# Attention inside a fused transformer block: output products issued one step later, two banks for transposed weights, three one-bank score tiles, two gates dealt out by halves

## The chip, the cores and the metric

The kernel runs on one NeuronCore of one Trainium2 chip. The metric is the time of one execution in microseconds, as the device measures it. Beside it stands one profiled execution, from which all traces here come. Engines are named as the profile names them: PE (TensorE, matrix products; PEld is its weight load), DVE (VectorE), ACT (ScalarE), POOL (GpSimd) and SP (SyncE, which only issues transfers here).

## The reference

One layer of a hybrid encoder, on 1024 tokens of 1024 channels, in float32. Cut to what matters:

```python
h    = rmsnorm(x, g_pre_mix)
proj = h @ w_in                                  # [u_pool 512 | q 512 | k 512 | v 512]
y_pool = multiscale_pool(u_pool, ...) @ w_br_pool
# stick-breaking attention, 8 heads of 64, strictly causal
z    = (q @ k.T) * 64 ** -0.5
A[t,s] = sigmoid(z_ts) * prod_{s<j<t} (1 - sigmoid(z_tj))      # s < t
y_sb = (A @ v) @ w_br_sb
gates  = sigmoid(h @ w_gate + b_gate)            # 2048 channels
merged = gates[:1024] * y_pool + gates[1024:] * y_sb
x = x + rmsnorm(merged @ w_out, g_post_mix)
x = x + rmsnorm(relu(rmsnorm(x, g_pre_mlp) @ w_up) ** 2 @ w_down, g_post_mlp)
```

## The kernel before, in words

Every float32 operand of a product is split into a high and a low part of a narrower type (`hi` by a cast on ACT, `lo` by a subtraction on DVE), and a product is three matmuls: hi·hi, lo·hi, hi·lo (`mm3`, lines 108 to 114; a row of L110 or L112 is the first of the three). Activations lie with channels on the 128 partitions and tokens along the row, in two halves of 512 tokens. Weights come as 128x1024 tiles through `prep` (L76 load, L82 cast, L83 subtraction).

Stages, in order:

1. **phase_in** (0 to 78 us): x is loaded and split unnormalized; the sums of squares go through a matmul with a matrix of ones (`stats`, tile `ms`, L332), then `rstd` (L153 Ln and L154 Exp on ACT, L155 to L157 on DVE) makes the row factors `rb[h]` of each half, and four transposes of `rb[h]` (tile `rt`, L336) with a copy (L337) make the same factors per column. `u` (tiles `du`, `zu`), then the first q and k and the pooling mixer (`win`, `dm`, `yscr`) follow. `u_out` (L380) multiplies a finished u product with `rb` and frees its bank.
2. **phase_attention** (78 to 503 us): for each of 8 heads, four groups g = 3, 2, 1, 0 of two query blocks i = 2g and 2g+1. `att_scores` makes the scores z of one block (w = 128(i+1) columns, two matmuls for each piece of up to 512), T = sigmoid(z) and F = sigmoid(-z) on ACT (L551, L552), a running product over F on DVE (L559, the scan) and its product with T (L560), which is the attention row block. F has one buffer, so the F of a block waits for L560 of the block before. `att_out` of the group before then goes through its steps m = 0..g: transposes of the weights (tile `at`, L576), a split into `ahi` (ACT, L583) and `alo` (DVE, L584), and four matmuls into `o` (L589: ahi twice, alo twice); at the end of a group `o` is folded into `oT` (L593, L594).
   Between these, `pump` deals out the head's **fillers**: steps of the gate products (`dg`, three matmuls a step, 8 steps for each half gate), of the next q and k (`dqk`) and of v (`dv`). `self.fill` lists which fillers belong to which head: head 4 has two gates (32 steps), heads 5, 6 and 7 have 48.
3. **phase_post** and **phase_mlp** (503 us to the end): branch products, output projection, norms, and the MLP by a seven-product scheme.

PSUM has eight banks of 128x512 f32. Before: `d` two, score tiles `z` two of two banks each, `o` one, `at` one.

What sets the order: the code is written in one sequence, and a list scheduler at build time reorders instructions between engines by its own estimates; within an engine the built order is then fixed. While `pin` is set, the first matmul of a triple is held behind the fourth last entry of `marks` (scores, transposes, output products).

The lines that the change and the prediction's steps touch:

Of the kernel before, what the change touches and what calls it, by code (L numbers as in the profile page):

```python
# [29 lines left out]
P = 128  # L30
# [19 lines left out]
class Block:  # L50
# [118 lines left out]
    def build(self):  # L169
# [78 lines left out]
    def phase_in(self):  # L248
# [81 lines left out]
        def stats(h):  # L330
            ms = self.zps.tile([P, H], F32, name="ms", tag="at" if h == 0 else "o", bufs=1)
            nc.tensor.matmul(ms, self.ones, accs[h], start=True, stop=True)  # L332
            self.rstd(ms, pa, ("sq", 3), out=self.rb[h])
            rt = self.zps.tile([P, H], F32, name="rt", tag="at", bufs=1)
            for j in range(4):
                nc.tensor.transpose(rt[:, j * P : j * P + P], self.rb[h][:, j * P : j * P + P], self.eye)  # L336
# [70 lines left out]
        def pool_mix(g, cur):  # L407
# [6 lines left out]
            for h in range(2):  # L414
                c = slice(h * H, h * H + H)
                d = self.zps.tile([P, H], F32, name="dm", tag=("o", "at")[h], bufs=1)
# [111 lines left out]
    def att_scores(self, h, i):  # L528
# [9 lines left out]
        z = self.zps.tile([P, 1024], F32, name="z", tag="z", bufs=2)  # L538
        pieces = [(0, max(256, min(H, w)))]
        if w > H:  # L540
            pieces.append((H, max(256, w - H)))
        tt = slice(i * P, i * P + P)
        for c, n in pieces:
            m = nc.tensor.matmul(z[:, c : c + n], q[:, tt], k[:, c : c + n], start=True, stop=False)  # L544
            if c == 0:
                self.marks.append(m)
            nc.tensor.matmul(z[:, c : c + n], qs[:, tt], k[:, c : c + n], start=False, stop=True)  # L547
# [3 lines left out]
        nc.scalar.activation(tl[:, :w], z[:, :w], AF.Sigmoid)  # L551
        nc.scalar.activation(f[:, :w], z[:, :w], AF.Sigmoid, scale=-1.0)  # L552
# [10 lines left out]
    def att_out(self, h, g, a):  # L563
# [3 lines left out]
        hd = (h % 4) * P  # L567
        for m in range(g + 1):
            diag = m == g
            at = self.zps.tile([P, H], F32, name="at", tag="at", bufs=1)  # L570
# [14 lines left out]
            for part in (hi, lo):  # L585
                for s, c in ((2 * m + 1, 0), (2 * m, 256)):
                    v = self.v[(h // 4, s)].rearrange("p h x -> p (h x)")[:, hd : hd + P]
                    first = m == 0 and c == 0 and part is hi
                    t = nc.tensor.matmul(o, v, part[:, c : c + 256], start=first, stop=diag and c == 256 and part is lo)  # L589
            self.marks.append(t)  # L590
# [22 lines left out]
    def phase_attention(self):  # L613
# [6 lines left out]
        self.w_out = 2.3  # L620
        self.pin = True
# [34 lines left out]
        self.att_out(*prev)  # L656
        while self.queue:
            self.advance()
# [645 lines left out]
```

## Time and profile before

| | |
|---|---|
| time, median of 3 runs | 1307.06 us (1303.7 to 1307.58) |
| profiled execution | 1308.59 us, of which the trace's span is 1306.8 us |
| PE busy | 1278.9 us (98%) |
| DVE busy | 915.6 us (70%) |
| ACT busy | 600.7 us (46%) |
| POOL busy | 173.8 us (13%) |
| mean granted PE clock | 0.993 |

PE is busy 98% of the span. Idle time of PE is what the trace shows directly; beside it the column PEclk of a stage tells whether PE ran at its full clock there. DVE, ACT and POOL only count where PE waits for them. Matmul ends are modelled in the trace (pipelined matmuls overlap), so rates are read from start to start: 0.23 us for a 128x512 matmul, 0.12 us for a 128x256 one.

### The profile page before, as it was taken

The page shows a single profiled execution, that of the slowest core. Times are in us where ns is not written, and L with a number is a line of the kernel's source. Part 1 is how long each engine was busy: PE and PEld are TensorE (multiplying, and loading weights), DVE is VectorE, ACT ScalarE, POOL GpSimd, SP SyncE. Part 2 cuts the span into 40 slices and gives each one's busy share as a digit, 9 for nine tenths or more (in the row PEclk, how much of TensorE's full clock was granted, in tenths as well). Part 3 has the DMA queues.
Part 4 walks back from the last instruction along what each step waited for, and adds up shares of the span by engine and source line. Part 5 has one row for each costly group of instructions (what it writes and reads, how often), then busy time and mean ns, then how long its engine had stood idle before and what let it go on. Part 6 is the DMA issues. An engine that isn't in the chain of part 4 may idle for free.

```text
span 1306.8 us, 16746 instructions
## 1 busy us (share of the span) xinstructions
PE 1278.9 (98%) x6145; PEld 1066.9 (82%) x6145; DVE 915.6 (70%) x1239; ACT 600.7 (46%) x925; POOL 173.8 (13%) x346
## 2 busy tenths in 40 slices
PE   9999999998999999999999999999999999999996
PEld 6888888887888888888878878888888888888886
DVE  8785587676777765663586869877775655776976
ACT  7244455544555543223355646544465433344341
POOL 1002213201212331100001001211121000001100
PEclk9998999999999999999999999999999999999998
DMA  6243635623746979543156667765559555556741
GB/s 221 71 155 113 204 103 155 136 66 73 154 147 191 251 230 240 166 170 104 54 188 229 189 227 251 251 229 184 188 211 354 180 185 202 193 178 240 241 166 65
DMA packets 75746, 233.72 MB, mean 179 GB/s; under 512 B 8624, under 2 KB 11184, under 8 KB 73488
## 3 DMA queue, kind: packets, MB, share of 16 engines
q1 hardware_dynamic: 47936, 143.64, 33.5%
q0 software_dynamic: 27152, 88.49, 22.7%
q8 instruction: 48, 0.79, 0.2%
q10 hardware_dynamic: 576, 0.52, 0.1%
q14 instruction: 34, 0.28, 0.1%
HBM read 178.10 MB, written 83.89 MB: 200 GB/s over the span
## 4 chain that ended last, share of the span: by engine, by line
PE 84%; DVE 8%; ACT 3%; DMA 2%; issue 2%; POOL 1%; SPq 0%; DVEq 0%; ACTq 0%; POOLq 0%
PE d L113 19%; PE d L114 19%; PE d L112 19%; PE dg L110 4%; PE dg L113 4%; PE dg L114 4%; PE o L589 2%; PE at L576 2%; DVE F L559 2%; DVE T L560 1%; PE dqk L114 1%; PE dqk L113 1%; DMA yscr<-win 1%; PE z L547 1%; PE z L544 1%
## 5 line engine op out<-in xcount | busy, mean ns | idle before, releaser
L113 PE MATMUL d<-blo,whi 128*128 128x512 f32 (+1 forms) x456 | 172.7, 379 | 0.0
L114 PE MATMUL d<-bhi,wlo 128*128 128x512 f32 (+1 forms) x456 | 171.9, 378 | 0.0
L112 PE MATMUL d<-bhi,whi 128*128 128x512 f32 (+1 forms) x456 | 168.6, 378 | 0.0
L559 DVE TENSOR_TENSOR_SCAN F<-F,past 128x896 f32<-128x896 f32 (+3 forms) x64 | 87.6, 1369 | 46.9 <-ACT F L552 46.5
L82 ACT CAST whi<-wraw 128x512 fp32r<-128x512 f32 (+1 forms) x88 | 67.6, 797 | 86.4 <-PE d L113 37.5
L110 PE MATMUL dg<-hT_hi,whi 128*128 128x512 f32 x256 | 105.3, 411 | 0.0
L114 PE MATMUL dg<-hT_hi,wlo 128*128 128x512 f32 x256 | 101.0, 394 | 0.0
L113 PE MATMUL dg<-hT_lo,whi 128*128 128x512 f32 x256 | 100.7, 393 | 0.0
L83 DVE TENSOR_TENSOR wlo<-wraw,whi 128x512 fp32r<-128x512 f32 (+1 forms) x88 | 77.8, 907 | 30.5 <-ACT whi L82 30.3
L114 PEld LDWEIGHTS d<-bhi,wlo 128*128 128x128 f32 x456 | 85.8, 188 | 16.1 <-issue 0.2
L113 PEld LDWEIGHTS d<-blo,whi 128*128 128x128 f32 x456 | 85.7, 188 | 16.1 <-issue 0.2
L112 PEld LDWEIGHTS d<-bhi,whi 128*128 128x128 f32 x456 | 85.5, 188 | 16.1
L584 DVE TENSOR_TENSOR alo<-at,ahi 128x512 fp32r<-128x512 f32 (+1 forms) x80 | 50.3, 629 | 43.2 <-ACT ahi L583 42.5
L113 PE MATMUL d<-b_lo,whi 128*128 128x512 f32 x196 | 76.7, 392 | 0.0
L112 PE MATMUL d<-b_hi,whi 128*128 128x512 f32 x196 | 75.7, 391 | 0.0
L114 PE MATMUL d<-b_hi,wlo 128*128 128x512 f32 x196 | 75.3, 392 | 0.1
L1071 DVE TENSOR_TENSOR wlo<-slots_hi,whi 128x1024 fp32r<-128x1024 f32 x29 | 35.5, 1225 | 53.8 <-ACT whi L1069 53.8
L1069 ACT CAST whi<-slots_hi 128x1024 fp32r<-128x1024 f32 x29 | 30.5, 1052 | 84.6 <-PE d L113 64.7
L583 ACT CAST ahi<-at 128x512 fp32r<-128x512 f32 (+1 forms) x80 | 43.5, 544 | 47.5 <-PE at L576 44.2
L1069 ACT CAST whi<-slots_lo 128x1024 fp32r<-128x1024 f32 x27 | 28.4, 1052 | 72.9 <-PE d L113 59.2
L1071 DVE TENSOR_TENSOR wlo<-slots_lo,whi 128x1024 fp32r<-128x1024 f32 x27 | 33.0, 1222 | 36.7 <-ACT whi L1069 36.7
L114 PEld LDWEIGHTS dg<-hT_hi,wlo 128*128 128x128 f32 x256 | 48.3, 189 | 10.5
(305 smaller groups left out, 3325.9 us busy)
## 6 DMA issues: line engine op xcount, KB each, us to landing
wraw<-w SPq DMA_DIRECT2D x80, 512.0 KB, 4.2
wscr<-w POOLq DMA_DIRECT2D x24, 1024.0 KB, 10.3
ext_b<-ascr SPq DMA_DIRECT2D x40, 512.0 KB, 4.4
gscr<-gs POOLq DMA_DIRECT2D x32, 256.0 KB, 4.1
gate<-gscr POOLq DMA_DIRECT2D x16, 512.0 KB, 3.7
pscr<-p SPq DMA_DIRECT2D x32, 256.0 KB, 3.6
braw<-w SPq DMA_DIRECT2D x16, 512.0 KB, 5.5
ascr<-c POOLq DMA_DIRECT2D x32, 256.0 KB, 5.1
```

The lines of the kernel that those rows point to most:

```text
L82: nc.scalar.copy(hi[:, c], raw[:, c])
L83: self.last_lo = nc.vector.tensor_sub(lo[:, c], raw[:, c], hi[:, c].bitcast(F32)).ins
L110: nc.tensor.matmul(ps, wh, rh, start=first and i == 0, stop=False)
L112: nc.tensor.matmul(ps, wh, rh, start=first and i == 0, stop=False)
L113: nc.tensor.matmul(ps, wh, rl, start=False, stop=False)
L114: nc.tensor.matmul(ps, wl, rh, start=False, stop=last and i == n - 1)
L559: nc.vector.tensor_tensor_scan(fr, fr, past, 1.0, ALU.mult, ALU.max)
L576: t = nc.tensor.transpose(at[:, b * P : b * P + P], a[tt][:, s * P : s * P + P], self.eye)
L583: nc.scalar.copy(hi[:, c0:], at[:, c0:])
L584: nc.vector.tensor_sub(lo[:, c0:], at[:, c0:], hi[:, c0:].bitcast(F32))
L1069: last_split[0] = nc.scalar.copy(hi, src).ins
L1071: last_split[1] = nc.vector.tensor_sub(lo, src, hi.bitcast(F32)).ins
```

## The change

Five things change.

- **Output products one step later.** The four `o` matmuls of a step are no longer issued at the end of that step. `att_out` keeps them as `pending`, and the next step (of the same group or of the next one) issues them through `att_products` after its own transposes, fillers and split. Folding `o` into `oT` moves along. After the last group an explicit `pump` and `att_products` finish.
- **`at` has two banks**, so transposes of a step can be written while those of the step before are still being split.
- **`z` is three tiles of one bank** instead of two of two banks. A block with w > 512 becomes two tiles, and the order is now matmuls, T and F of the first 512 columns, then matmuls, T and F of the rest. The scan still runs over the whole row.
- **Consequences in phase_in**: of the six u accumulators that used the score banks, three take `z` tiles and one an `at` bank; `ms` and `rt` of both halves now share the single `o` bank; `dm` of the second half may use either `at` bank.
- **Gates 4 and 12 by halves**: the first half of gate 4 moves from head 5 to head 4, the first half of gate 12 from head 6 to head 5. Head 4 has 40 filler steps, head 5 still 48, head 6 has 40.

```diff
-            4: [("g", 3), ("g", 11)],
-            5: [("q", 3), ("k", 3), ("g", 4)],
-            6: [("g", 12), ("g", 5), ("g", 13)],
+            4: [("g", 3), ("g", 11), ("g", 4, 0)],
+            5: [("g", 4, 1), ("q", 3), ("k", 3), ("g", 12, 0)],
+            6: [("g", 12, 1), ("g", 5), ("g", 13)],
...
         def stats(h):
-            ms = self.zps.tile([P, H], F32, name="ms", tag="at" if h == 0 else "o", bufs=1)
+            ms = self.zps.tile([P, H], F32, name="ms", tag="o", bufs=1)
...
-            rt = self.zps.tile([P, H], F32, name="rt", tag="at", bufs=1)
+            rt = self.zps.tile([P, H], F32, name="rt", tag="o", bufs=1)
...
-        z0 = self.zps.tile([P, 1024], F32, name="zu0", tag="z", bufs=2)
-        z1 = self.zps.tile([P, 1024], F32, name="zu1", tag="z", bufs=2)
         d2 = [self.dps.tile([P, H], F32, name="du", tag="d") for _ in range(2)]
-        dst = [d2] + [[z[:, h * H : h * H + H] for h in range(2)] for z in (z0, z1)]
+        zu = [self.zps.tile([P, H], F32, name="zu", tag="z", bufs=3) for _ in range(3)]
+        zu.append(self.zps.tile([P, H], F32, name="zu", tag="at", bufs=2))
+        dst = [d2, zu[:2], zu[2:]]
...
+        for c in range(0, w, H):
+            n = min(H, w - c)
+            cols = slice(c, c + max(256, n))
+            z = self.zps.tile([P, H], F32, name="z", tag="z", bufs=3)
+            zz = z[:, : max(256, n)]
+            m = nc.tensor.matmul(zz, q[:, tt], k[:, cols], start=True, stop=False)
+            if c == 0:
+                self.marks.append(m)
+            nc.tensor.matmul(zz, qs[:, tt], k[:, cols], start=False, stop=True)
+            nc.scalar.activation(tl[:, c : c + n], z[:, :n], AF.Sigmoid)
+            nc.scalar.activation(f[:, c : c + n], z[:, :n], AF.Sigmoid, scale=-1.0)
...
-            at = self.zps.tile([P, H], F32, name="at", tag="at", bufs=1)
+            at = self.zps.tile([P, H], F32, name="at", tag="at", bufs=2)
...
             nc.vector.tensor_sub(lo[:, c0:], at[:, c0:], hi[:, c0:].bitcast(F32))
-            for part in (hi, lo):
-                for s, c in ((2 * m + 1, 0), (2 * m, 256)):
...
-            self.marks.append(t)
+            self.att_products()
+            self.pending = (h, g, m, o, hi, lo)
+
+    def att_products(self):
+        if self.pending is None:
+            return
+        h, g, m, o, hi, lo = self.pending
+        self.pending = None
+        diag = m == g
+        for part in (hi, lo):
+            for s, c in ((2 * m + 1, 0), (2 * m, 256)):
...
+        self.marks.append(t)
+        if not diag:
+            return
...
         self.att_out(*prev)
+        self.pump(self.w_out)
+        self.att_products()
```

How the built order moves, at three places. A name with a number is one tile; the bracket names the engines for which an instruction has to wait.

PE in head 4, just after the first scores of the head, before: transposes of a diagonal step, nine filler matmuls, scores, and then that step's four products.

```order
L576 MATMUL at_2961<-eye_159,T_2770 128x128 [waits PE_49]
L576 MATMUL at_2961<-eye_159,T_2748 128x128
...
L114 MATMUL dg_3005<-hT_hi0_249,wlo_2599 128x512
L544 MATMUL z_3062<-k4_2595,q4_2467 128x512 [waits Activation_49]
L547 MATMUL z_3062<-k4_2595,qs4_2588 128x512
L544 MATMUL z_3062<-k4_2595,q4_2467 128x256
L547 MATMUL z_3062<-k4_2595,qs4_2588 128x256
L589 MATMUL o_2931<-ahi_2962,v0_3_1040 128x256 [waits Activation_49,Pool_49]
L589 MATMUL o_2931<-ahi_2962,v0_2_1068 128x256
L589 MATMUL o_2931<-alo_2963,v0_3_1040 128x256 [waits DVE_49,Pool_49]
```

The same step after: `at_3007` are its transposes, `o_2974` with `ahi_3008` and `alo_3009` its products.

```order
L575 MATMUL at_3007<-eye_159,T_2810 128x128 [waits PE_49]
...
L547 MATMUL z_3068<-k4_2635,q4_2501 128x512
L550 MATMUL z_3068<-k4_2635,qs4_2628 128x512
L575 MATMUL at_3097<-eye_159,T_2952 128x128 [waits DVE_49]
...
L547 MATMUL z_3073<-k4_2635,q4_2501 128x512 [waits Activation_49]
...
L600 MATMUL o_2974<-ahi_3008,v0_3_1048 128x256 [waits Activation_49,Pool_49]
L600 MATMUL o_2974<-ahi_3008,v0_2_1076 128x256
L600 MATMUL o_2974<-alo_3009,v0_3_1048 128x256 [waits DVE_49,Pool_49]
L547 MATMUL z_3128<-k4_2635,q4_2501 128x512 [waits Activation_49]
```

Between the transposes and the first alo product stood 9 filler and 4 score matmuls and the two ahi products; now another step's transposes, 24 `dv` and 24 `dg` matmuls, score matmuls and another step's products stand there too.

ACT at the first two-tile block of head 0, before: one T and one F over 1024 columns, F behind DVE.

```order
L551 ACTIVATE T_888<-z_883 128x1024
L496 ACTIVATE v0_2_1068<-dv_1043,rcol_167 128x4x64 [waits PE_49]
L496 ACTIVATE v0_1_1096<-dv_1071,rcol_167 128x4x64 [waits PE_49]
L552 ACTIVATE F_889<-z_883 128x1024 [waits DVE_49,Activation_49]
L551 ACTIVATE T_1132<-z_1127 128x640 [waits PE_49]
```

After: two of each.

```order
L551 ACTIVATE T_888<-z_890 128x512
L496 ACTIVATE v0_2_1076<-dv_1051,rcol_167 128x4x64 [waits PE_49]
L551 ACTIVATE T_888<-z_895 128x512 [waits PE_49]
L552 ACTIVATE F_889<-z_890 128x512 [waits DVE_49,Activation_49]
L552 ACTIVATE F_889<-z_895 128x512
```

Each block of more than 512 columns has one T and one F more on ACT, 64 instructions in all; where the second score tile comes later, its T stands behind the F of the first.

PE in phase_in, at the end of the u products, before: `ms_463` (the sums of the second half) stands among the u products, and the transposes `rt_471` of its row factors come 28 u matmuls and four transposes later.

```order
L332 MATMUL ms_463<-acc_292,ones_152 128x512 [waits DVE_49,PE_49]
L114 MATMUL zu0_331<-hT_hi1_290,wlo_188 128x512
...
L336 MATMUL rt_421<-eye_159,rb0_165 128x128 [waits DMAHW1_49,DVE_49]
L336 MATMUL rt_421<-eye_159,rb0_165 128x128 x3
L112 MATMUL zu1_332<-hT_hi1_290,whi_190 128x512
...
L114 MATMUL zu1_332<-hT_hi1_290,wlo_191 128x512
L336 MATMUL rt_471<-eye_159,rb1_166 128x128 [waits DVE_49,PE_49]
L336 MATMUL rt_471<-eye_159,rb1_166 128x128 x3
L112 MATMUL du_544<-hT_hi0_249,whi_484 128x512 [waits DVE_49,Activation_49]
```

After:

```order
L336 MATMUL rt_423<-eye_159,rb0_165 128x128 [waits DMAHW1_49,DVE_49]
L336 MATMUL rt_423<-eye_159,rb0_165 128x128 x3
...
L112 MATMUL zu_336<-hT_hi1_290,whi_190 128x512
L332 MATMUL ms_465<-acc_292,ones_152 128x512 [waits DVE_49]
L113 MATMUL zu_336<-hT_lo1_291,whi_190 128x512
L114 MATMUL zu_336<-hT_hi1_290,wlo_191 128x512
L336 MATMUL rt_473<-eye_159,rb1_166 128x128 [waits DVE_49]
L336 MATMUL rt_473<-eye_159,rb1_166 128x128 x3
L112 MATMUL du_546<-hT_hi0_249,whi_486 128x512 [waits DVE_49,Activation_49]
```

`ms_465` now stands behind the first half's transposes and copy (the shared `o` bank), and two matmuls separate it from `rt_473`, which needs its result.

More of the change, by code (lines that the diff above doesn't have):

```diff
@@ L415, in pool_mix @@
                 c = slice(h * H, h * H + H)
-                d = self.zps.tile([P, H], F32, name="dm", tag=("o", "at")[h], bufs=1)
+                d = self.zps.tile([P, H], F32, name="dm", tag=("o", "at")[h], bufs=h + 1)
                 self.mm3(d, [(wmh[:, g, :], wml[:, g, :], ph[:, c], pq[:, c])])
@@ L537, in att_scores @@
         w = (i + 1) * P
[L538 to L547, printed above, removed]
         odd = i // 2 % 2
@@ L584, in att_out @@
             nc.vector.tensor_sub(lo[:, c0:], at[:, c0:], hi[:, c0:].bitcast(F32))
[L585 to L590 removed]
+            self.att_products()
+            self.pending = (h, g, m, o, hi, lo)
+    def att_products(self):
+        nc = self.nc
+        if self.pending is None:
[3 more added lines that the diff above has]
+        diag = m == g
+        hd = (h % 4) * P
+        for part in (hi, lo):
+            for s, c in ((2 * m + 1, 0), (2 * m, 256)):
+                v = self.v[(h // 4, s)].rearrange("p h x -> p (h x)")[:, hd : hd + P]
+                first = m == 0 and c == 0 and part is hi
+                t = nc.tensor.matmul(o, v, part[:, c : c + 256], start=first, stop=diag and c == 256 and part is lo)
+        self.marks.append(t)
+        if not diag:
+            return
         b = 64 * (h % 2)
```

5 lines of the change are left out of this document (2 added, 3 removed).

## The prediction

> **What bounds the kernel now.** I read the page's first part, then PE in stages (the table of windows), then who PE waited for, then the timeline at the places those name.
>
> ```profile
> PE 1278.9 (98%) x6145; PEld 1066.9 (82%) x6145; DVE 915.6 (70%) x1239; ACT 600.7 (46%) x925; POOL 173.8 (13%) x346
> ```
>
> PE is the bound, so the change, which keeps every matmul, can only win what PE loses by standing still or by running at half clock. The windows of the attention stage (columns: length, then busy us of PE, PEld, DVE, ACT, POOL, then the granted PE clock) say how much that is:
>
> ```profile
> 104.20:107.60 3.40, 1.55 (x9) 1.06 (x8) 2.02 (x1) 2.99 (x5) 1.36 (x2) 1.00 0.00 0
> 107.60:111.00 3.40, 2.16 (x9) 1.95 (x10) 2.94 (x5) 1.62 (x2) 0.52 (x2) 0.50 0.00 0
> 111.00:114.40 3.40, 3.40 (x18) 3.40 (x18) 3.30 (x4) 1.14 (x2) 1.32 (x1) 0.50 0.00 0
> ...
> 310.00:319.20 9.20, 7.75 (x40) 6.23 (x38) 7.30 (x7) 4.32 (x8) 2.78 (x4) 1.00 0.19 39
> 319.20:322.60 3.40, 1.60 (x9) 1.22 (x10) 3.02 (x3) 0.83 (x2) 0.00 (x0) 1.00 1.12 204
> 322.60:326.00 3.40, 3.40 (x12) 2.82 (x11) 0.88 (x2) 0.59 (x1) 0.00 (x0) 0.50 0.44 79
> ...
> 360.00:503.00 143.00, 142.31 (x742) 120.68 (x741) 94.58 (x130) 70.27 (x126) 40.55 (x87) 1.00 0.74 206
> sum 425.00, PE 413.43 PEld 355.32 DVE 291.51 ACT 209.97 POOL 97.24; mean PE 37.58 PEld 32.30 DVE 26.50 ACT 19.09 POOL 8.84
> ```
>
> From 78 to 503 us PE is idle 425.00 - 413.43 = 11.6 us. Twice, right after a 3.4 us window in which PE was busy less than half (1.55 and 1.60 us), the clock falls to 0.50, for two windows and for one. Late in attention (360 on) almost nothing is lost, so there is nothing to win there. Who PE waited for:
>
> ```profile
> PE o L589 <- DVE alo L584: 4.7, 9, 1.4
> PE z L544 <- ACT F L552: 3.1, 4, 1.9
> PE at L576 <- DVE T L560: 2.3, 1, 2.3
> ```
>
> These are 10.1 of the 11.6 us, in 14 stops. One of each kind, PE with the DVE or ACT row that made it late:
>
> ```profile
> 105.60 0.50 PE L544 MATMUL z<-k,q 128*128 128x512 f32 x1 [0.81 <-ACT F L552]
> 108.84 0.47 PE L576 MATMUL at<-eye,T 128*128 128x128 f32 x1 [2.28 <-DVE T L560]
> 305.45 2.02 DVE L559 TENSOR_TENSOR_SCAN F<-F,past 128x896 f32<-128x896 f32 x1 [0.85 <-ACT F L552]
> 306.27 0.40 PE L589 MATMUL o<-ahi,v 128*128 128x256 f32 x2
> 307.39 0.53 DVE L584 TENSOR_TENSOR alo<-at,ahi 128x384 fp32r<-128x384 f32 x1
> 308.07 0.47 PE L589 MATMUL o<-alo,v 128*128 128x256 f32 x2 [1.39 <-DVE alo L584]
> 318.74 0.81 ACT L552 ACTIVATE F<-z 128x768 f32<-128x768 f32 x1 [1.85 <-DVE T L560]
> 319.60 0.50 PE L544 MATMUL z<-k,q 128*128 128x512 f32 x1 [1.86 <-ACT F L552]
> ```
>
> The third to sixth rows are the disease that the change treats: `alo` sits behind a 2.02 us scan on DVE, and PE, having nothing between, waits 1.39 us. From 306.27 to 308.07 two matmuls of 0.12 us pass: 1.80 - 0.24 = 1.56 us are lost, 0.17 more than the idle shown, since ends are modelled. So 14 stops cost 14 x 0.17 = 2.4 us more. Half clock costs half of PE's busy time in the three windows at 0.50: (2.16 + 3.40 + 3.40)/2 = 4.5 us. Waits too short to show stretch the alo products:
>
> ```profile
> L589 PE MATMUL o<-alo,v 128*128 128x256 f32 x160 | 34.8, 299 | 4.9 <-DVE alo L584 4.7
> L589 PE MATMUL o<-alo,v x160: 277/283/388, 130.3 to 501.6; 128*128 128x256 f32 x160
> ```
>
> Mean 299 against median 283 ns, x 160 = 2.6 us. All that attention loses: 11.6 + 2.4 + 4.5 + 2.6 = **21.1 us**. That is the ceiling of the gain.
>
> **The change part by part.**
>
> *Products one step later, two `at` banks.* No matmul is added; `at` writes can run ahead by one step. The distance on PE between a step's last transpose and its first alo product, counted in the built order at 0.23, 0.12 and (transposes) 0.09 us a matmul, has a mean of 3.6 us before and 8.0 after, its smallest value 1.0 before and 4.0 after. What has to fit into it is a cast, a subtraction, and at worst one scan ahead of them:
>
> ```profile
> L583 ACT CAST ahi<-at 128x512 fp32r<-128x512 f32 x48 | 28.1, 585 | 42.9 <-PE at L576 41.9
> L584 DVE TENSOR_TENSOR alo<-at,ahi 128x512 fp32r<-128x512 f32 x48 | 33.1, 689 | 40.1 <-ACT ahi L583 39.7
> L559 DVE TENSOR_TENSOR_SCAN F<-F,past 128x1024 f32<-128x1024 f32 x8 | 18.3, 2290 | 1.9 <-ACT F L552 1.7
> ```
>
> 0.59 + 0.69 + 2.29 = 3.6 us, under 4.0. So the o waits go in full: 4.7 + 9 x 0.17 + 2.6 = 8.8 us. DVE's own queue doesn't get shorter by it; what is late next is the chain of F, below. The end of the stage has its last products behind twelve branch matmuls, which cover them; bounds 0 and 12 x 0.23 = 2.8 us, taken 0.
>
> *Head 0's start.* The transposes that waited 2.28 us at 108.84 now stand behind 24 more matmuls; z's 0.81 us stop goes as F of a first half is done before the whole F was. I count both, their 2 x 0.17, and the two half-clock windows ((2.16 + 3.40)/2 = 2.8): 6.2 us gained.
>
> *Gates 4 and 12 by halves.* The 8 steps moved are 24 matmuls, 24 x 0.23 = 5.5 us of cover for head 4, where the 1.86 us stop and, through the stop after it, the half clock of 322.6 arose; total work is unchanged, and the first half's gate evictions, its write to `gscr` and one weight-sum transfer on POOL's queue move with them (POOL is busy 97.24 of 425 us). Gained: 1.86 + 0.17 + 1.7 = 3.7 us. Head 6 falls to 40 steps, as head 4 now has; its cover of before is gone by 5.5 us, and I price that with the next item.
>
> *Three one-bank score tiles.* A T or F over 1024 columns becomes two over 512:
>
> ```profile
> L551 ACT ACTIVATE T<-z 128x1024 f32<-128x1024 f32 x8 | 8.4, 1047 | 2.1 <-PE z L547 2.1
> L551 ACT ACTIVATE T<-z 128x512 f32<-128x512 f32 x8 | 5.0, 629 | 0.0
> L552 ACT ACTIVATE F<-z 128x512 f32<-128x512 f32 x8 | 4.8, 595 | 4.1 <-DVE T L560 4.0
> ```
>
> 2 x 629 - 1047 = 0.21 us for each of 64 instructions: 13.5 us of ACT, spread over 425 us of which ACT works 210; hidden as such. On the path of F it is not: ACT is a queue in order, and behind L560 of the block before it now may have F, T, F (0.60 + 0.63 + 0.60 = 1.82 us) where it had one F of 1.05 us. So the chain F, scan, L560 grows by up to 0.8 us in each of 4 blocks a head, 3.2 us a head. The bounds: nothing (PE has cover in six heads, as the row 360:503 shows), and 8 x 3.2 = 25.6 us where it is last everywhere. I take it as last in part in the two heads of 40 steps, near the row of head 4 (DVE busy 7.30 of 9.20): 4 us, new stops and their starts included.
>
> *Stats on one bank.* This is the cost I hold for largest. Rows of before, from `ms` of the second half to the first use of its factors:
>
> ```profile
> 35.26 1.02 PE L332 MATMUL ms<-acc,ones 128*128 128x512 f32 x2
> 36.32 0.69 ACT L153 ACTIVATE rb<-ms,eps 128x512 f32<-128x512 f32 x1 [3.89 <-PE ms L332]
> 37.02 1.05 ACT L82 CAST whi<-wraw 128x1024 fp32r<-128x1024 f32 x1
> 37.97 0.63 ACT L154 ACTIVATE rb<-rb 128x512 f32<-128x512 f32 x1
> 39.24 0.68 DVE L155 SCALAR_TENSOR_TENSOR nb<-ms,rb 128x512 f32<-128x512 f32 x1
> 40.69 0.69 DVE L157 SCALAR_TENSOR_TENSOR rb<-nb,rb 128x512 f32<-128x512 f32 x1
> 41.30 1.28 DVE L380 TENSOR_TENSOR u<-du,rb 128x512 f32<-128x512 f32 x2
> 42.76 0.39 PE L114 MATMUL zu<-hT_hi,wlo 128*128 128x512 f32 x1
> 42.99 0.60 PE L336 MATMUL rt<-eye,rb 128*128 128x128 f32 x4
> 43.34 0.48 PE L112 MATMUL du<-hT_hi,whi 128*128 128x512 f32 x1
> ```
>
> The factors are ready at 40.69 + 0.69 = 41.38, 6.1 us after `ms` began; PE did u products meanwhile. In the built order of after the cast still stands between Ln and Exp, but PE has only `ms` (0.86: its 1.02 less the 0.16 us by which ends run over) and two matmuls (0.46) before `rt`. `rt` (0.35) then starts 6.1 us after `ms`, and the next product waits for the bank that L380 frees 6.7 us after `ms`. PE would have been there at 0.86 + 0.46 + 0.35 = 1.7 and gets there at 6.9: **5.2 us lost**, PE idle some 4.7. Without the cast and the subtraction beside it the chain is 1.06 + 0.69 + 0.63 + 2.14 = 4.5 us and the loss 3.6; with the cast itself late by the two matmuls' 0.46 us and its own queue, some 6.0. And the clock: the edges of its windows in the rows above lie 3.41 us apart (107.6, 111.0, 114.4; 322.6 is 63 of them after 107.6), so they also fall at 42.7, 46.15, 49.55 and 53.0. `ms` would begin at 43.34 - 1.7 = 41.7, PE be idle from 43.2 to 47.9, so the window from 42.7 is almost empty and half clock follows at 46.15, for one window or two. As after 107.6 I take two: PE busy from 47.9 to 53.0 at half, 2.5 us lost (one window: 0.8).  What follows on DVE (`u_out`, the pooling) starts later by about as much as PE does, so I give nothing back. In sum 7.7 us; bounds 3.6 (short chain, clock up) and 8.5.
>
> Here a page can be weighed. The rows say that a window less than half busy is enough for half clock (1.55 of 3.40, 1.60 of 3.40). The Trainium skill, "TensorE: Matmul & The Clock Gate", section "Part 1: The HAM clock gate", puts the cold state after at least one idle window of about 3.4 us, free-running. Taken literally no window of the new stop is wholly idle, the clock would stay, and the sum would lack the 2.5 us; the two falls in this trace speak against it.
>
> **Sum.** Gained 8.8 + 6.2 + 3.7 = 18.7; lost 4 + 7.7 = 11.7; net 7.0 gained. Of the rest of the ceiling (21.1 - 18.7 = 2.4 us, small stops in heads 1 to 3) I count half, 1.2: 8.2 us in all. The profiled execution took 1308.59 us, so 1300.4; the median of the runs is 1.5 lower, hence **1299 us**.
>
> **The rivals.**
>
> *F's chain becomes the bound (slower).* Place: each head's first two groups; mechanism: the second tile of block 2g+1 needs the bank that F of the first tile of block 2g frees, and that F waits for L560 of the block before. Price 3.2 us a head; it decides from three heads on beyond my 4 us. For it: DVE already waits for F in those heads, and PE did wait for F four times. Against: PE had cover in six heads. In six heads: 1299 + 6 x 3.2 - 4 = 1314.
>
> *The clock stays up in phase_in.* For it: the two windows of the new stop are each touched by some busy time (0.5 and 1.7 us). Against: 1.55 of 3.40 wasn't enough twice. 1299 - 2.5 = 1296.5, with the short chain as well 1295.
>
> *The stop is short and nothing new stops.* With 3.6 us in phase_in and half clock for one window (0.8), the whole ceiling gained and no stop by F: 1299 - 3.3 - 1.2 - 4 = 1290.5.
>
> *Waits only change their name.* Where DVE is at 7.30 of 9.20, PE waits for scores or transposes instead of `alo`. Then the gain is head 0's and half of the o waits, 6.2 + 4.4 = 10.6, against 11.7 lost: 1307 + 1.1 = 1308, no change.
>
> **How the numbers follow.** My forecast (half clock and the stop as summed, 1297 to 1303) 0.45; the clock stays up (1294 to 1297) 0.10; short stop and nothing new (1288 to 1294) 0.13; waits renamed 0.18; F's chain 0.14. 0.3% is 3.9 us and about what a measurement of this kernel tells from no change. Faster takes the first three, 0.68; same is the fourth and a piece of the fifth, 0.21; slower 0.11. The range leaves out the far end of F's chain and the lowest part of the third case: 1290 to 1309.
>
> **What would show it.** Right: PE's waits of `o` for `alo` are gone; a PE stop of 4 to 5 us at `rt` near 43 us with PEclk 0.5 after it; no half clock at 108 and 322; ACT 64 instructions more and some 13 us busier; F's wait for T longer. Wrong: no stop at 43 us; several stops of z for F, or of `at` for T, in heads 4 and 6 or in every head; PE clock low in attention again.

## The result and the profile after

The changed kernel takes **1292.46 us** (median of 5 runs, 1291.42 to 1293.4) against 1306.85 us before (median of 5, 1303.7 to 1307.58): ratio 0.9895 [0.9882, 0.9908], 14.4 us faster. The forecast was 1299. The profiled execution took 1291.99 us, its span 1290.3; before it was 1308.59, 1.7 above the median.

First the page's line of busy time, after. PE, which is the bound, lost 10.8 us of busy time and still runs the same 6145 matmuls; ACT has the 64 instructions more. Since the matmuls are the same, the 10.8 us were half clock and matmuls stretched by waits too short to show as idle time.

```profile
PE 1268.1 (98%) x6145; PEld 1063.1 (82%) x6145; DVE 915.3 (71%) x1239; ACT 604.7 (47%) x989; POOL 168.1 (13%) x346
```

Who PE waited for, from 0 to 515 us of the changed kernel (total us, times, longest). The 14 stops of `o`, `z` and `at` shown before are gone but for one of 0.3 us at `at`. A new one leads, `rt`; a small one, `d`, closes attention.

```profile
PE rt L336 <- DVE rb L157: 4.6, 1, 4.6
...
PE d L112 <- DVE oT L607: 0.9, 1, 0.9
PE dg L110 <- DVE v L497: 0.6, 1, 0.6
...
PE at L575 <- DVE T L560: 0.3, 1, 0.3
```

The new stop in the timeline of the changed kernel (start, duration, engine; the bracket is the idle time before). Read it as the chain named in the prediction: `ms`, Ln (L153), the weight cast in between (L82), Exp (L154), three DVE instructions, `rt`.

```profile
42.63 1.02 PE L332 MATMUL ms<-acc,ones 128*128 128x512 f32 x2
...
43.69 0.69 ACT L153 ACTIVATE rb<-ms,eps 128x512 f32<-128x512 f32 x1 [5.52 <-PE ms L332]
43.73 0.40 PE L114 MATMUL zu<-hT_hi,wlo 128*128 128x512 f32 x1
44.28 1.03 ACT L82 CAST whi<-wraw 128x1024 fp32r<-128x1024 f32 x1
45.21 0.63 ACT L154 ACTIVATE rb<-rb 128x512 f32<-128x512 f32 x1
...
46.49 0.68 DVE L155 SCALAR_TENSOR_TENSOR nb<-ms,rb 128x512 f32<-128x512 f32 x1
...
47.20 0.69 DVE L156 TENSOR_TENSOR nb<-nb,rb 128x512 f32<-128x512 f32 x1
47.93 0.69 DVE L157 SCALAR_TENSOR_TENSOR rb<-nb,rb 128x512 f32<-128x512 f32 x1
...
48.68 0.91 PE L336 MATMUL rt<-eye,rb 128*128 128x128 f32 x4 [4.55 <-DVE rb L157]
...
49.37 0.77 PE L112 MATMUL du<-hT_hi,whi 128*128 128x512 f32 x1
```

From `ms` to the first product behind `rt` pass 49.37 - 42.63 = 6.74 us, where PE's own work is 1.67: 5.1 us lost.

Stages of the changed kernel (length; busy us of PE, PEld, DVE, ACT, POOL; the granted clock). The five short rows follow the clock's windows of 3.41 us; one was at half speed after the new stop, and one near the start, where before had none. The long row is attention and the first branch products.

```profile
4.57:7.98 3.41, 2.15 (x8) 0.79 (x6) 2.92 (x4) 1.99 (x4) 1.96 (x2) 1.00 0.88 251
7.98:11.39 3.41, 3.02 (x7) 1.87 (x7) 2.64 (x6) 2.89 (x8) 0.00 (x0) 0.50 1.04 403
...
42.12:45.53 3.41, 2.00 (x7) 0.96 (x6) 0.19 (x1) 1.84 (x3) 0.00 (x0) 1.00 0.12 48
45.53:48.94 3.41, 0.26 (x2) 0.26 (x3) 3.34 (x5) 0.31 (x1) 0.00 (x0) 1.00 0.37 95
48.94:52.35 3.41, 3.41 (x11) 2.68 (x10) 3.41 (x9) 0.00 (x0) 0.00 (x0) 0.50 0.15 59
...
78.00:503.00 425.00, 422.75 (x2369) 366.68 (x2368) 301.40 (x411) 218.52 (x446) 94.99 (x210) 1.00 0.62 166
```

PE's idle time from 78 to 503 fell from 11.6 us to 425.00 - 422.75 = 2.25, and the clock stood at 1.00 throughout. For the balance I took every start-to-start gap of PE's matmuls less what such a matmul takes when PE runs on (0.23 us for 512 columns, 0.17 for 384, 0.12 for 256, 0.11 for 128; 0.43 for the two-byte 512). That counts idle time, hidden ends and half clock together. The levels hang on the third decimal of these times (0.228 for 512 columns; with 0.229 the 3.8 below would be 2.6), the differences between two kernels hardly do:

| us lost by PE | before | after |
|---|---|---|
| 0 to 78 (phase_in) | 3.4 | 10.8 |
| 78 to 115 (head 0 begins) | 7.4 | 0.6 |
| 115 to 503 | 18.5 | 3.8 |
| 503 to 515 | 0.7 | -0.1 |
| 515 to the end | 2.5 | 0.8 |

Attention gave 25.9 - 4.4 = 21.5 us, phase_in took back 7.4, the rest (0.8 + 1.7) gave 2.5: 16.6 in all, which is 1308.59 - 1291.99. The 1.7 lie in stages that the change does not touch; there the traces of all thirteen kernels lose between 0.7 and 2.5 us, so I put it down to the execution and not to the change.

Last, groups of the changed kernel (busy us, mean ns | idle time before, by what it ended). The alo products have lost their stretch (299 to 282 ns). F's wait for T (L560 of the block before), which was to grow, is 30.6 us against 28.9 before, and the scan's wait for F fell from 46.5 to 39.6. T and F together are busy 93.9 us against 83.9 before.

```profile
L559 DVE TENSOR_TENSOR_SCAN F<-F,past 128x896 f32<-128x896 f32 (+3 forms) x64 | 87.0, 1360 | 40.4 <-ACT F L552 39.6
...
L551 ACT ACTIVATE T<-z 128x512 f32<-128x512 f32 (+2 forms) x96 | 47.2, 494 | 30.0 <-PE z L550 16.1 <-PE at L575 11.8 <-POOL alo L581 1.5
L552 ACT ACTIVATE F<-z 128x512 f32<-128x512 f32 (+2 forms) x96 | 46.7, 492 | 30.8 <-DVE T L560 30.6
...
L600 PE MATMUL o<-alo,v 128*128 128x256 f32 x160 | 32.1, 282 | 0.0
```

### The profile page after: what moved, and what is told of

It reads as the page before. It is cut to its first block, busy times and chain, and to the rows that moved or that the text cites. A ratio compares the mean times of both kernels' runs of the same rounds, so it can differ in the third digit from the quotient of the medians.

```text
span 1290.3 us, 16786 instructions
## 1 busy us (share of the span) xinstructions
PE 1268.1 (98%) x6145; PEld 1063.1 (82%) x6145; DVE 915.3 (71%) x1239; ACT 604.7 (47%) x989; POOL 168.1 (13%) x346
## 4 chain that ended last, share of the span: by engine, by line
PE 94%; DVE 4%; ACT 1%; issue 1%; DMA 0%; SPq 0%; DVEq 0%; ACTq 0%
PE d L112 20%; PE d L114 20%; PE d L113 20%; PE dg L110 4%; PE dg L114 4%; PE dg L113 4%; PE o L600 3%; PE at L575 2%; PE dqk L113 2%; PE dqk L114 2%; PE dqk L110 2%; PE z L550 1%; PE z L547 1%; PE dv L114 1%; PE dv L113 1%
## 5 line engine op out<-in xcount | busy, mean ns | idle before, releaser
L559 DVE TENSOR_TENSOR_SCAN F<-F,past 128x896 f32<-128x896 f32 (+3 forms) x64 | 87.0, 1360 | 40.4 <-ACT F L552 39.6
L82 ACT CAST whi<-wraw 128x512 fp32r<-128x512 f32 (+1 forms) x88 | 67.7, 802 | 85.7 <-PE d L113 35.1
L112 PEld LDWEIGHTS d<-bhi,whi 128*128 128x128 f32 x456 | 85.5, 188 | 15.9
L583 DVE TENSOR_TENSOR alo<-at,ahi 128x512 fp32r<-128x512 f32 (+1 forms) x80 | 50.3, 630 | 32.6 <-ACT ahi L582 31.4
L551 ACT ACTIVATE T<-z 128x512 f32<-128x512 f32 (+2 forms) x96 | 47.2, 494 | 30.0 <-PE z L550 16.1
L552 ACT ACTIVATE F<-z 128x512 f32<-128x512 f32 (+2 forms) x96 | 46.7, 492 | 30.8 <-DVE T L560 30.6
```

What stands on the lines that cost most here:

```text
L82: nc.scalar.copy(hi[:, c], raw[:, c])
L112: nc.tensor.matmul(ps, wh, rh, start=first and i == 0, stop=False)
L551: nc.scalar.activation(tl[:, c : c + n], z[:, :n], AF.Sigmoid)
L552: nc.scalar.activation(f[:, c : c + n], z[:, :n], AF.Sigmoid, scale=-1.0)
L559: nc.vector.tensor_tensor_scan(fr, fr, past, 1.0, ALU.mult, ALU.max)
L583: nc.vector.tensor_sub(lo[:, c0:], at[:, c0:], hi[:, c0:].bitcast(F32))
```

## The experiments

All times are medians, all ratios against the kernel before run in the same group on the same chip (its medians there: 1306.45 to 1306.57). Where two changed kernels are compared, they may have run on different chips; the medians of the kernel before differ by 0.4 us between all groups.

### Which half of "one step later, two banks" carries the gain?

**The changed kernel with one `at` bank** (its fourth u accumulator and `dm` then share that bank):

```diff
-        zu.append(self.zps.tile([P, H], F32, name="zu", tag="at", bufs=2))
+        zu.append(self.zps.tile([P, H], F32, name="zu", tag="at", bufs=1))
...
-                d = self.zps.tile([P, H], F32, name="dm", tag=("o", "at")[h], bufs=h + 1)
+                d = self.zps.tile([P, H], F32, name="dm", tag=("o", "at")[h], bufs=1)
...
-            at = self.zps.tile([P, H], F32, name="at", tag="at", bufs=2)
+            at = self.zps.tile([P, H], F32, name="at", tag="at", bufs=1)
```

> The changed kernel with one at bank instead of two (one bank left empty); three one-bank score tiles, later products, gates by halves and the stop at rt stay. Theory, as the runs so far suggest (the second at bank is what pays; with one, the next step's transposes wait for alo, 6.7 to 7.5 us in 14 or 15 stops): 1292.5 + 12 = 1303 to 1307. Rival (the one-bank score tiles pay): 1293 to 1296.

Measured 1309.13 us, ratio 1.0016 [1.0007, 1.0025]: the whole gain is gone and 16.7 us lie between one bank and two. By start-to-start gaps the loss is in attention, where PE loses some 21 us from 78 to 503 against 4.4 in the changed kernel; phase_in, in which the shared bank also serves `u` and `dm`, loses no more than there. PE's waits in this kernel, 78 to 503 us:

```profile
PE at L575 <- DVE alo L583: 7.2, 13, 1.8
PE o L600 <- ACT ahi L582: 1.8, 4, 0.8
PE o L600 <- DVE oT L607: 1.2, 1, 1.2
PE at L575 <- DVE T L560: 0.8, 1, 0.8
```

Before, PE waited for `alo` at the product; here it waits for the same subtraction (L583) one place earlier, at the next step's transposes, because that subtraction is what frees the only `at` bank. The wait has changed its name and its size is no smaller (4.7 before, 7.2 now).

**The kernel before with the products one step later and nothing else** (with the new `att_products` and, after the last group, `pump` and `att_products`; one `at` bank, the old score tiles):

```diff
-            for part in (hi, lo):
-                for s, c in ((2 * m + 1, 0), (2 * m, 256)):
...
+            self.att_products()
+            self.pending = (h, g, m, o, hi, lo)
```

> The kernel before, with output products one step later and nothing else. Theory (later products remove the o waits): 8.8 us faster, 1298. Rival (with one at bank the next transposes wait for alo instead: mean distance to the alo products 4.8 us, smallest 0.7): 3 to 5 us faster, 1302 to 1304, with stops of at or o in its place.

Measured 1308.0 us, ratio 1.0007 [0.9997, 1.0016]: nothing gained. The leading waits are the same two kinds, with `at` for `alo` at the head:

```profile
PE at L575 <- DVE alo L583: 6.7, 14, 0.9
PE at L575 <- DVE T L560: 2.3, 1, 2.3
PE o L600 <- DVE oT L607: 2.0, 5, 0.7
PE o L600 <- ACT ahi L582: 1.5, 3, 0.5
```

**The changed kernel on all the old banks**: two score tiles of two banks, one `at` bank, `ms`, `rt` and the u accumulators placed as before. What is left of the change is the later products and the gates by halves:

```diff
-            at = self.zps.tile([P, H], F32, name="at", tag="at", bufs=2)
+            at = self.zps.tile([P, H], F32, name="at", tag="at", bufs=1)
...
+        z = self.zps.tile([P, 1024], F32, name="z", tag="z", bufs=2)
...
+        nc.scalar.activation(tl[:, :w], z[:, :w], AF.Sigmoid)
+        nc.scalar.activation(f[:, :w], z[:, :w], AF.Sigmoid, scale=-1.0)
```

> The changed kernel with products one step later and gates by halves, but the banks of before: two two-bank score tiles, one at bank, ms and rt where they were, no stop at rt. Theory (later products do the work, banks cost the stop): 1292.5 - 6 for the stop, + 3 for steps that one at bank holds close (mean distance 4.9 us, smallest 1.0): 1289. Rival (banks do the work): o waits and head 0's stops stay, 1299 to 1302.

Measured 1306.87 us, ratio 1.0001 [0.9992, 1.0011]; `at` waits for `alo` 15 times, 7.5 us. Three kernels with one `at` bank, three times no gain.

**The changed kernel with the products at their old place** (issued at the end of their own step):

```diff
-            self.att_products()
             self.pending = (h, g, m, o, hi, lo)
+            self.att_products()
```

> The changed kernel with all banks and gates, but each step's output products issued in their own step again. Theory of the prediction (products one step later are what removes the o waits): the o waits come back, 8.8 us, 1301. Rival (the second at bank is enough, since the scheduler may then run transposes ahead: the mean distance from transposes to alo products is 5.3 us in the built order against 8.0 with the change and 3.6 before, the smallest 3.5): under 3 us slower, 1293 to 1295.

Measured 1293.65 us, ratio 0.9906 [0.9893, 0.992], against 0.9895 [0.9882, 0.9908] for the whole change: with two banks the old place of the products costs 1.2 us at the medians, and the intervals overlap. The built order explains why it is so little. The distance on PE between a step's last transpose and its first alo product, counted as in the prediction, has a mean of 5.3 us here and a smallest value of 3.5 (before 3.6 and 1.0; changed kernel 8.0 and 4.0; the two changed kernels with one `at` bank 4.9 and 1.0). With a second bank the scheduler can pull the next transposes ahead by itself; the products need not be moved in the code for that. The trace differs at two places. The half clock after the stop at `rt` lasts two windows here, which costs 0.7 us more than in the changed kernel; and at the end of attention this kernel's longest wait after `rt` is

```profile
PE d L112 <- ACT oh L713: 1.7, 1, 1.7
```

where the changed kernel has 0.9.

### What do the shared statistics cost?

**The changed kernel with `ms` of the second half in an `at` bank**, so that it need not wait for the first half's `rt` and its copy:

```diff
-            ms = self.zps.tile([P, H], F32, name="ms", tag="o", bufs=1)
+            ms = self.zps.tile([P, H], F32, name="ms", tag=("o", "at")[h], bufs=h + 1)
```

> The changed kernel, with the sums of the second half (`ms`) in the at bank that is free in phase_in instead of the shared o bank. Theory (the stop at rt is a plain loss): the 4.55 us stop and the one half-clock window behind it (some 1.3 us) go, 1292.5 - 6 = 1286 to 1287, ratio to before 0.985. Rival (given back: with phase_in 6 us shorter the first T of head 0 is again late by the pooling's transfers, as before the change, with 3.1 us of stops and half clock there): 1290 to 1293, with stops near 100 us.

Measured **1284.74 us** (1284.32 to 1285.41), ratio 0.9836 [0.9822, 0.9849]: 7.7 us less than the changed kernel. It beats both kernels. The timeline of it shows Ln, cast and Exp as before, now with products beside them, and `rt` without a wait:

```profile
35.59 0.69 ACT L153 ACTIVATE rb<-ms,eps 128x512 f32<-128x512 f32 x1 [3.89 <-PE ms L332]
36.30 1.05 ACT L82 CAST whi<-wraw 128x1024 fp32r<-128x1024 f32 x1
37.25 0.63 ACT L154 ACTIVATE rb<-rb 128x512 f32<-128x512 f32 x1
...
42.25 0.60 PE L336 MATMUL rt<-eye,rb 128*128 128x128 f32 x4
42.60 0.48 PE L112 MATMUL du<-hT_hi,whi 128*128 128x512 f32 x1
```

Little of the stop is given back in attention: PE loses 1.6 us from 78 to 115 here, against 0.6 behind the stop.

**The kernel before with `ms` and `rt` of both halves in the `o` bank**, and nothing else:

```diff
-            ms = self.zps.tile([P, H], F32, name="ms", tag="at" if h == 0 else "o", bufs=1)
+            ms = self.zps.tile([P, H], F32, name="ms", tag="o", bufs=1)
...
-            rt = self.zps.tile([P, H], F32, name="rt", tag="at", bufs=1)
+            rt = self.zps.tile([P, H], F32, name="rt", tag="o", bufs=1)
```

> The kernel before, with ms and rt of both halves in the one o bank and nothing else changed. Theory (plain loss): a stop of 4.6 us at rt and one half-clock window, 1307 + 6 = 1313. Rival (given back): the pooling's transfers then land earlier against PE, head 0's 3.1 us of stops and its half clock (2.8 us) go, 1306 to 1308.

Measured 1308.64 us, ratio 1.0019 [1.001, 1.0029]: slower by only 2.1 us, although the stop is there in full. Its waits:

```profile
PE rt L336 <- DVE rb L157: 4.5, 1, 4.5
PE o L589 <- DVE alo L584: 4.5, 8, 1.4
PE z L544 <- ACT F L552: 2.2, 3, 1.9
```

and its first part of attention, to be held against 7.4 us lost there before:

```profile
78.00:115.00 37.00, 36.55 (x251) 33.66 (x250) 26.51 (x38) 17.97 (x27) 5.54 (x9) 1.00 0.43 136
```

By start-to-start gaps 1.1 us are lost here. The stops at the head's beginning and the half clock after them are gone; my reading is that PE comes later into head 0 while DVE and ACT have had time to get ahead. By that reading a stop just ahead of a place where PE waits anyway is partly free; once that place is mended, as in the changed kernel, it costs its full price.

### Do the one-bank score tiles cost or bring anything?

**The changed kernel with two one-bank score tiles instead of three** (four of the six u accumulators lie outside the `d` banks; two of these now take the score tiles and two the `at` banks; one of the eight banks stays unused):

```diff
-        zu = [self.zps.tile([P, H], F32, name="zu", tag="z", bufs=3) for _ in range(3)]
-        zu.append(self.zps.tile([P, H], F32, name="zu", tag="at", bufs=2))
+        zu = [self.zps.tile([P, H], F32, name="zu", tag="z", bufs=2) for _ in range(2)]
+        zu += [self.zps.tile([P, H], F32, name="zu", tag="at", bufs=2) for _ in range(2)]
...
-            z = self.zps.tile([P, H], F32, name="z", tag="z", bufs=3)
+            z = self.zps.tile([P, H], F32, name="z", tag="z", bufs=2)
```

> The changed kernel with two one-bank score tiles instead of three (one bank left empty). It asks from where F's chain becomes the bound. Theory: the second tile of a block then waits for F of the first tile of the same or the former block, which waits for L560 of the block before; some 2 us in each of the two large groups of 8 heads, 1292 + 16 to 32 = 1308 to 1324, with stops of z for F. Rival (the scheduler finds filler for them, as it did with three): under 5 us slower.

Measured 1292.83 us, ratio 0.9892 [0.9878, 0.9905]: no cost. Taking a third of the score room away makes the chain of F no longer at any place that PE feels; the scan's wait for F is 36.2 us.

**The version with the free `ms` bank, its score room one tile of two banks**, with T and F over the whole row as before the change (so as many banks for scores as in the last kernel, but one tile; one u accumulator takes the bank that becomes free):

```diff
+        z = self.zps.tile([P, 1024], F32, name="z", tag="z", bufs=1)
...
+        nc.scalar.activation(tl[:, :w], z[:, :w], AF.Sigmoid)
+        nc.scalar.activation(f[:, :w], z[:, :w], AF.Sigmoid, scale=-1.0)
```

> The kernel with ms in the free at bank (1284.7 us) and one score tile of two banks instead of three of one: T and F go over the whole row again. Theory (two at banks pay, the shape of the score tiles does not): 1285 to 1288. Rival (F's chain: with one tile the next block's scores wait for the F of this one, which waits for L560 of the last): stops of z for F of about 2 us in each head, 1300.

Measured 1292.37 us, ratio 0.9890 [0.9876, 0.9903], 7.6 us above the kernel that it was made from. Its waits show where a part of that goes, and its long row that 425.00 - 418.76 = 6.2 us are idle from 78 to 503 (2.0 in the kernel it came from). By start-to-start gaps 10.9 us are lost there against 4.5, 6.4 of the 7.6:

```profile
PE z L544 <- ACT F L552: 2.2, 2, 1.8
...
PE at L575 <- DVE alo L583: 1.2, 2, 0.7
```

```profile
78.00:503.00 425.00, 418.76 (x2340) 361.89 (x2339) 298.06 (x405) 214.06 (x379) 97.63 (x209) 1.00 0.60 161
```

One-bank tiles therefore seem to have a worth of their own when score room is scarce: the first half's F frees one bank while the second half is still being worked on. It is shown by two pairs only: the kernel with the free `ms` bank has three one-bank tiles, and that a third tile brings nothing was seen in the changed kernel, where the stop at `rt` stands ahead; two one-bank tiles with the free `ms` bank were not run.

### The gates by halves

**The changed kernel with gates 4 and 12 whole**, in heads 5 and 6 as before:

```diff
-            4: [("g", 3), ("g", 11), ("g", 4, 0)],
-            5: [("g", 4, 1), ("q", 3), ("k", 3), ("g", 12, 0)],
-            6: [("g", 12, 1), ("g", 5), ("g", 13)],
+            4: [("g", 3), ("g", 11)],
+            5: [("q", 3), ("k", 3), ("g", 4)],
+            6: [("g", 12), ("g", 5), ("g", 13)],
```

> The changed kernel with gates 4 and 12 dealt out whole, as before. Theory of the prediction (8 more steps in head 4 are worth its 1.86 us stop and its half clock): 3.7 us slower, 1296. Rival (later products and the new banks cover head 4 with 32 steps as well): within 1 us of 1292.5, no stop of PE in head 4.

Measured 1292.01 us, ratio 0.9892 [0.9878, 0.9905]: no difference to the changed kernel. PE stands still 425.00 - 422.67 = 2.3 us from 78 to 503, as with the halves; head 4's stop stays away without them.

```profile
78.00:503.00 425.00, 422.67 (x2367) 366.40 (x2366) 300.85 (x411) 219.40 (x445) 97.37 (x209) 1.00 0.62 166
```

**The kernel before with those gates by halves**, the same edit turned round:

```diff
-            4: [("g", 3), ("g", 11)],
+            4: [("g", 3), ("g", 11), ("g", 4, 0)],
...
```

> The kernel before, with gates 4 and 12 by halves and nothing else. Theory: head 4's 1.86 us stop and its half clock go, 3.7 us, 1303. Rival: head 6, now with 40 steps, stops instead of head 4: 1306 to 1307.

Measured 1301.48 us (1300.9 to 1304.84), ratio 0.9966 [0.9954, 0.9979]: 5.1 us at the medians, alone. Part of that is the stop it was aimed at: no `z` waits for F, and `o` waits for `alo` 2.7 us, 6 times, instead of 4.7, 9 times. Another part is the clock in the execution seen: head 0's stop at the transposes is still there, and the clock stays up behind it.

```profile
106.95 0.33 PE L576 MATMUL at<-eye,T 128*128 128x128 f32 x1 [2.27 <-DVE T L560]
```

The clock's windows of this execution, two that share the stop and the next:

```profile
102.28:105.69 3.41, 2.33 (x16) 1.82 (x14) 2.00 (x1) 3.02 (x5) 1.34 (x2) 1.00 0.00 0
105.69:109.11 3.42, 2.10 (x15) 1.91 (x16) 2.96 (x5) 1.66 (x3) 0.54 (x2) 1.00 0.00 0
109.11:112.52 3.41, 3.41 (x23) 3.08 (x22) 3.31 (x4) 3.11 (x7) 1.32 (x1) 1.00 0.00 0
```

How the 5.1 us divide between the two was not separated by a run. The five executions give a hint: three took 1300.9 to 1301.48 us with a mean granted clock of 0.996 to 0.997, two 1304.62 and 1304.84 us with 0.994 and 0.995, and the 21 of the kernel before beside them have 0.992 to 0.995. By that some 2 us are the stop and some 3 the clock; that is an estimate, not a measurement of either.

### Banks alone

**The kernel with the free `ms` bank, its gates whole and its products at their old place**: the kernel before plus the new banks and their one-bank score tiles (what is left of the rest is the explicit `pump` after the last group). Against the best version:

```diff
-            4: [("g", 3), ("g", 11), ("g", 4, 0)],
+            4: [("g", 3), ("g", 11)],
...
-            self.att_products()
             self.pending = (h, g, m, o, hi, lo)
+            self.att_products()
```

> The kernel before with the new banks alone: two at banks, three one-bank score tiles, ms of the second half in the free at bank; products in their own step, gates whole. Theory (banks are the whole gain, later products are worth the 1.2 us that not_later showed, gates nothing): 1286 to 1287. Rival (without later products and without halves head 4 stops again, since the distance to the alo products is 5.2 us in the mean and 2.9 at the least): 1290 to 1293.

Measured 1288.93 us, ratio 0.9862 [0.9849, 0.9876]: 17.5 of the 21.8 us by which the best version beats the kernel before come from the banks alone. The remaining 4.2 us belong to the later products and the halves together (ratios 0.9862 [0.9849, 0.9876] against 0.9836 [0.9822, 0.9849], touching at their ends); which of the two was not separated. By start-to-start gaps 2.4 us lie between 78 and 503 us. One piece is seen: the stop at the end of attention is 1.7 us here and 0.9 there.

## Why the prediction was right, and where its steps were off

**The o waits, 8.8 us: the size was right, the reason half right.** They went in full, idle time and stretch (282 ns, below the 283 of the median). The prediction gave the gain to products and banks together and counted the distance in the built order; the runs show that the second bank carries it. With one bank the later products gain nothing, and with two they add 1.2 us that the intervals do not separate from nothing. "Waits only change their name", a rival at 0.18, is exactly what happens with one bank.

The Trainium skill, "Perfetto Trace Analysis", section "Optimizing Tensor Performance", has independent groups of matmuls rotate through different banks, so that emptying one overlaps the next group. The runs agree: 16.7 us between one `at` bank and two. The same page of the Trainium skill, section "Matmul Optimizations", wants all eight banks in use. The runs do not bear that out as a rule by itself: seven banks gave 1292.83 us with one score tile less and 1309.13 with one `at` bank less, eight gave 1292.46.

**Head 0's start, 6.2 us: right in size.** Lost from 78 to 115 were 7.4 us before, 0.6 after, 1.6 without the stop in phase_in, and 2.0 with the banks alone: 5.4 by the banks. In the changed kernel the stop in phase_in may have done as much, since the kernel before with the shared statistics loses 1.1 there. But the half clock in it (2.8) is not in every execution: a stop of 2.27 us at the same place passed without it above. The kernel before spreads from 1303.5 to 1309.5 us over its 56 runs, the best version from 1284.3 to 1285.4 over only four, and the profiled execution of before lay high in its spread.

**Gates by halves, 3.7 us: wrong inside this change, 0.** The rest of the change removes head 4's stop without them; added to the kernel before they bring 5.1, a part of it that stop. The prediction treated the stop as theirs alone. The sum did not suffer, since the stop went all the same.

**Three one-bank score tiles, 4 us lost: wrong, 0.** The step that failed is "I take it as last in part in the two heads of 40 steps". The splitting itself is there (10.0 us more of T and F, where 13.5 were counted), but no `z` waits for F in any head, the scan waits less for F than before, and even two tiles cost nothing. The prediction counted that F stands behind one more instruction, and left out of this term, though not of head 0's, that the first half's T and F start as soon as that half's scores are done and free their bank early. That this is the reason is my reading; what the runs show is that one wide tile on two banks costs 7.6 us against three one-bank tiles.

**Stats on one bank, 7.7 us lost: right.** Idle 4.55 us where some 4.7 were forecast, 5.1 lost by starts where 5.2 were, with the cast between Ln and Exp; undoing it brings 7.7 us. One part was off: half clock came for one window after the stop, not two. The six products from 49.37 to 52.07 took 2.70 us where six take 1.38 at 0.23, and `rt` 0.3 longer (already in the 5.1): 1.6 us in all where 2.5 were counted. Of the six kernels with this stop two show the two windows (gates whole and products at their old place), so either could come. Of the 7.4 us that phase_in lost by the trace, 6.9 lie between 40 and 52.4 us, 0.4 of them `ms` itself, which stood before 40 us in the kernel before; 0.5 came before 40 us, where another window ran slow in this execution. That undoing the stop brings the very 7.7 us forecast is partly luck, since the trace prices stop and half clock at 6.5.

The windows' edges, too, were met by luck. The prediction took them from the trace of before, and they came 0.6 us away from there; but from one execution to the next they lie anywhere. The first edge after the start, counted within the 3.41 us, falls between 0.08 and 3.30 us in the thirteen traces.

On that window the Trainium skill's rule ("TensorE: Matmul & The Clock Gate", section "Part 1: The HAM clock gate": at least one idle window) fares as it did in the prediction. The window 45.53 to 48.94 was empty but for 0.26 us, and half clock followed; so it did after 4.57 to 7.98, in which PE was busy 2.15 of 3.41 us. The rule taken literally allows neither. That the windows run freely, as the same section of the Trainium skill has it, agrees with those edges.

**The end of attention, taken as 0: 0.9 us.** The last products stand just ahead of the branch products, and PE waits for the last `oT`. It lies within the bounds of 0 and 2.8.

**Small stops, half of 2.4 counted: most went.** By the balance above 4.4 of 25.9 us remain in attention, the 0.9 at its end among them.

In sum the steps gave 8.2 us and the medians 14.4. Of the missing 6.2, attention gave 21.5 where the terms made 8.8 + 6.2 + 3.7 + 1.2 - 4 = 15.9: 5.6, of which 4 are the chain of F that did not come and the rest small stops. Phase_in took 0.3 less than forecast, the stages behind attention gave 2.5 that no term had, and 2.2 are to be taken off again because the two profiled executions lie 16.6 us apart, not 14.4. The nearest rival by time, "short stop and nothing new" at 1290.5, is right in its second half only: nothing new stops in attention, but the stop in phase_in was long. So the measured 1292.46 us lie in the 1288 to 1294 that this rival had at 0.13, and outside the 1297 to 1303 that the forecast gave itself at 0.45: the way and the large terms were right, and the sum was 6 us short. The "ceiling" of 21.1 us was no ceiling either: the balance finds 25.9 us lost in attention, since waits too short to show as idle time make 7.5 of it, where 2.6 were counted at the alo products alone; 21.5 of the 25.9 were won.

## What to carry to other kernels

When PE waits for the split of a transposed operand, look first at what frees the buffer that is written next: moving the consumer later only moves the wait until a second bank is there, and with a second bank the order may mend itself. Before a bank is taken from another stage, price the wait that this makes there: here one accumulator moved from a shared to a free bank was worth 7.7 us, more than half of what the whole change had gained. Terms that remove the same stop are not to be added, and a stop's price depends on whether the next stage would have waited anyway: the same 4.5 us of idle time cost 2.1 us in one kernel and 7.7 in the other.

## What the runs showed of the hardware

I had not expected how much hangs on where a stop falls among the clock's windows. Within a trace the changes of the clock lie whole multiples of 3.413 us apart (107.6 and 322.6 in the kernel before: 63 of them), and I took the windows on each trace's own grid, for all thirteen traces, from 30 us to 1265. Eleven windows at full clock were followed by half clock, and PE was busy 0.00 to 1.63 us of 3.41 in them. The least busy window that was not followed by it had 1.73 us (products at their old place, 493.03 to 496.44). At half clock four windows, with PE busy 1.50 to 2.16 us, were followed by another at half; those with 3.08 us or more by full clock.

So a stop of 2.3 us at head 0's transposes was followed by half clock in the kernel before, where a part of it and the scores' stop of 0.81 us left PE 1.57 us of work in one window, and not in the kernel before with gates by halves, where the two windows that share it had 2.33 and 2.10. The share of busy time sorts the windows in these traces, with the bound somewhere between 1.63 and 1.73 us. At the start it does not: 2.15 us (4.57 to 7.98) was followed by 0.50 in the changed kernel, and 2.07 us (4.29 to 7.70) by 1.00 in the one with whole gates. The short `idle` matmuls of a two-byte type run there; why it differs stays open.
